# A softmax with relative position bias: one DMA queue and hand-placed pieces, against a queue for loads and a queue for stores

## The chip, the cores and the metric

The kernel runs on one core of a Trainium2 chip. The metric is the device time of one execution in microseconds; the median of several runs counts. The chip's core has a VectorE (DVE), a ScalarE (ACT), a GpSimd (POOL), a TensorE (PE, not used here), a SyncE (SP) that here only issues transfers, and 16 DMA engines, which move data between HBM and the on-chip memory (SBUF) for all of them.

## The reference

```python
B, H, S, max_rel = 2, 8, 2112, 16
logits: [B, H, S, S] f32        rel_bias: [H, 2 * max_rel + 1] f32
rel = clip(pos[:, None] - pos[None, :], -max_rel, max_rel) + max_rel
logits = logits + rel_bias[:, rel][None]
logits = logits - logits.max(axis=-1, keepdims=True)
exp = np.exp(logits)
return exp / exp.sum(axis=-1, keepdims=True)
```

There are 2 x 8 x 2112 = 33,792 rows of 2112 numbers. Each is read once and written once: 285.5 MB each way.

## The kernel before

Partition p of the 128 owns 264 neighbouring rows (`ROWS`), so one head's 2112 rows lie on 8 partitions. The rows are worked through in 44 chunks (`N`) of 6 rows per partition (`R`); a chunk is one load of 128 x 50,688 bytes and one store of the same size. There are four buffers, X0 to X3 (`NBUF`), and chunk n uses buffer n mod 4. Only the rows around the diagonal see a bias that is not constant. A strip of it for four chunks is copied out of PSUM (`M`) into `F`.

For each chunk VectorE adds the bias and takes the negative maximum of each row (`add`), ScalarE takes the exponential with its sum (`exps`), and VectorE, after every three rows (`HALF`), forms the reciprocals and scales (`scale`). VectorE does add and scale of a chunk before it goes on to the next. `take(eng, sem, n)` makes an engine wait for a semaphore and count it down. `ld[b]` says that a load has landed in buffer b, `st[b]` that its store has landed, `scaled` counts scaled rows.

SyncE issues all large transfers, in an order that is written out: the loads of chunks 0 to 3, the store of chunk 0, and then in a loop the store of chunk k+1 (after its scales) and the load of chunk k+4 (after the store of chunk k has landed). The transfers share one queue, in that order.

Two chunks are stored otherwise. Of chunk 0, rows 0 and 1 of each partition are left out of the main store (line 300). Lines 290 to 295 (`parts`) issue eight small transfers for part of them, each with one partition per DMA engine on fewer or more engines (`AHEAD`), and GpSimd stores the rest by five indirect transfers (`pieces`, line 165), whose rows are picked out by index lists that it builds (`choose`). A piece is 2 rows, 16.9 KB. Of chunk 41 the last three rows are treated likewise (`BEHIND` and `LAST`), in pieces of 25.3 KB. So some DMA engines store a few pieces more, others fewer. GpSimd waits for `ready` before each set, and SyncE waits for `soft` at the end. The last chunk is stored in two halves, on `landed`.

Of the kernel before, what the change touches and what calls it, by code (L numbers as in the profile page):

```python
# [8 lines left out]
I32 = mybir.dt.int32  # L9
EXP = mybir.ActivationFunctionType.Exp  # L10
ALU = mybir.AluOpType
ENG = mybir.EngineType
# [3 lines left out]
def kernel(  # L16
# [6 lines left out]
    nc = tc.nc  # L23
    P = 128
    B, H, S, S2 = logits.shape
# [3 lines left out]
    ROWS = B * H * S // P  # L29
    PB = S // ROWS  # L30
    assert ROWS * P == B * H * S and PB * ROWS == S and PB == H == 8
    R = 6
    NBUF = 4
    STEP = R * NBUF
    N = ROWS // R
    HALF = R // 2
# [1 line left out]
    MW = S + ROWS - 1  # L38
    FW = S + STEP - 1
    BIG = 3.0e38  # L40
    LOW, HIGH = 32, 96
    A0, A1 = 0, 2
    AHEAD = [(LOW + i, 16 - 2 * i) for i in range(4)] + [(i, 8) for i in range(4)]
    FIRST = [
# [5 lines left out]
    ]  # L50
    Z0, Z1 = HALF, R
    BEHIND = [(LOW + i, 16) for i in range(4)]
    LAST = [
        (80, 0, 1, []),
        (48, 80, 1, list(range(16, 48))),
# [3 lines left out]
    ]  # L59
    FAR = 1 << 20  # L60
    for own, plan in ((AHEAD, FIRST), (BEHIND, LAST)):
        assert sorted([p + 4 * i for p, k in own for i in range(k)]
                      + [p0 + lap * i for n, p0, lap, keep in plan for i in keep]) == list(range(P))

    io = ctx.enter_context(tc.tile_pool(name="io", bufs=1))
    X = [io.tile([P, R * S], FP32, tag=f"X{b}", name=f"X{b}") for b in range(NBUF)]
# [2 lines left out]
    nmax = io.tile([P, STEP], FP32, tag="nmax", name="nmax")  # L69
    tot = io.tile([P, STEP], FP32, tag="tot", name="tot")  # L70
    rec = io.tile([P, STEP], FP32, tag="rec", name="rec")
    sel = io.tile([P, len(FIRST) + len(LAST)], I32, tag="sel", name="sel")
    ip = io.tile([P, 3, PB], I32, tag="ip", name="ip")
    ps = ctx.enter_context(tc.tile_pool(name="ps", bufs=1, space=bass.MemoryType.PSUM))
    M = ps.tile([P, 4096], FP32, tag="M", name="M")
# [5 lines left out]
    def rows(t, j, n):  # L81

        return bass.AP(tensor=t.tensor, offset=t.offset + j * S, ap=[[ROWS * S, P], [1, n * S]])

    with tc.tile_critical(no_gpsimd_drain=True):  # L85
        ld = [nc.alloc_semaphore(f"ld{b}") for b in range(NBUF)]
        st = [nc.alloc_semaphore(f"st{b}") for b in range(NBUF)]
        added = nc.alloc_semaphore("added")
        expd = nc.alloc_semaphore("expd")
        scaled = nc.alloc_semaphore("scaled")  # L90
# [1 line left out]
        rb = nc.alloc_semaphore("rb")  # L92
        idx = nc.alloc_semaphore("idx")
        dve = nc.alloc_semaphore("dve")
        ready = nc.alloc_semaphore("ready")
        pool = nc.alloc_semaphore("pool")
        soft = tc.alloc_semaphore("soft")
        main = nc.alloc_semaphore("main")
        landed = tc.alloc_semaphore("landed")

        def take(eng, sem, n):
            eng.wait_ge(sem, n).then_inc(sem, -n)  # L102


        def load(j, b):
            nc.sync.dma_start(out=X[b][:, :], in_=rows(logits, j, R)).then_inc(ld[b], 16)

        def store(j, b, s0=0, n=R, sem=None):
            take(nc.sync, scaled, n)
            nc.sync.dma_start(  # L110
                out=rows(out, j + s0, n), in_=X[b][:, s0 * S : (s0 + n) * S]
            ).then_inc(sem or st[b], 16)

# [22 lines left out]

        nc.gpsimd.iota(ip[:, 0], pattern=[[0, PB]], base=0, channel_multiplier=1).then_inc(idx, 1)
        nc.gpsimd.iota(ip[:, 2], pattern=[[1, PB]], base=0, channel_multiplier=0).then_inc(idx, 1)
        g = nc.gpsimd
        made = [0]  # L140

        def step(ins):
            made[0] += 1
            ins.then_inc(pool, 1)

        def choose(plan, w, unit, row):

            for n, p0, lap, keep in plan:
                col = sel[:, w : w + 1]
                step(g.iota(col, pattern=[[0, 1]], base=(p0 * ROWS + row) // unit, channel_multiplier=lap * ROWS // unit))  # L150
                a, b = (min(keep), max(keep)) if keep else (P, P)
                cuts = [(-a, 1, ALU.is_ge), (b, -1, ALU.is_ge)]
                cuts += [(-i, 1, ALU.not_equal) for i in range(a, b) if i not in keep]
                for base, mul, op in cuts:
                    g.wait_ge(pool, made[0])
                    step(g.affine_select(out=col, in_=col, pattern=[[0, 1]], base=base, channel_multiplier=mul,  # L156
                                         compare_op=op, fill=float(FAR)))
                w += 1

        def pieces(plan, w, unit, x, r0):  # L160

            blocks = out.rearrange("b h s t -> (b h s t)").rearrange("(n c) -> n c", c=unit * S)
            step_p = list(x.ap[0])[0]
            for n, p0, lap, keep in plan:
                g.indirect_dma_start(  # L165
                    out=blocks, out_offset=bass.IndirectOffsetOnAxis(ap=sel[0:n, w : w + 1], axis=0),
                    in_=bass.AP(tensor=x.tensor, offset=x.offset + p0 * step_p + r0 * S,
                                ap=[[lap * step_p, n], [1, unit * S]]),
                    in_offset=None, bounds_check=P * ROWS // unit - 1, oob_is_err=False,
                ).then_inc(soft, 16)  # L170
                w += 1

        choose(FIRST, 0, A1 - A0, A0)
        take(g, pool, made[0])
        made[0] = 0
        take(g, ready, 1)
        pieces(FIRST, 0, A1 - A0, X[0], A0)
        choose(LAST, len(FIRST), Z1 - Z0, (N - 3) * R + Z0)
        take(g, pool, made[0])
        take(g, main, 16 * (1 + len(AHEAD)))  # L180
        g.wait_ge(soft, 16 * len(FIRST))
        g.sem_inc(st[0], 16)
        take(g, ready, 1)
        pieces(LAST, len(FIRST), Z1 - Z0, X[(N - 3) % NBUF], Z0)

        SC = H * W
        mask = [F[:, SC + i * PB : SC + (i + 1) * PB] for i in range(9)]
        dp, dh, eq, hm, gt, le, lt, ra, rz = mask
# [66 lines left out]
        def exps(b):  # L255
            for r in range(b * R, (b + 1) * R):
                x = X[b][:, (r - b * R) * S : (r - b * R + 1) * S]
                take(nc.scalar, added, 1)
                nc.scalar.activation(  # L259
                    out=x, in_=x, func=EXP, scale=-1.0, bias=nmax[:, r : r + 1],  # L260
                    accum_out=tot[:, r : r + 1],
                ).then_inc(expd, 1)
# [11 lines left out]
        with nc.Fori(0, ROWS - STEP + 1, STEP, engines=[ENG.DVE]) as j:  # L274
            strip(j)
            take(v, dve, 1)
            for b in range(NBUF):
                add(b)
                scale(b)
        with nc.Fori(0, ROWS // STEP, 1, engines=[ENG.Activation]):  # L280
            for b in range(NBUF):
                exps(b)

        def parts(own, x, r0, r1, j, sem):

            step_p = list(x.ap[0])[0]
            for p, k in own:
                nc.sync.dma_start(  # L290
                    out=bass.AP(tensor=out.tensor, offset=out.offset + (p * ROWS + j + r0) * S,
                                ap=[[4 * ROWS * S, k], [1, (r1 - r0) * S]]),
                    in_=bass.AP(tensor=x.tensor, offset=x.offset + p * step_p + r0 * S,
                                ap=[[4 * step_p, k], [1, (r1 - r0) * S]]),
                ).then_inc(sem, 16)

        nc.sync.wait_ge(scaled, HALF)
        nc.sync.sem_inc(ready, 1)
        take(nc.sync, scaled, R)
        nc.sync.dma_start(out=rows(out, A1, R - A1), in_=X[0][:, A1 * S : R * S]).then_inc(main, 16)  # L300
        parts(AHEAD, X[0], A0, A1, 0, main)
        with nc.Fori(0, ROWS - 2 * STEP + 1, STEP, engines=[ENG.SP]) as j:
            for b in range(NBUF):
                store(j + (b + 1) * R, (b + 1) % NBUF)
                take(nc.sync, st[b], 16)
                load(j + (b + NBUF) * R, b)
        take(nc.sync, scaled, R)
        nc.sync.sem_inc(ready, 1)
        late = X[(N - 3) % NBUF]
        nc.sync.dma_start(out=rows(out, (N - 3) * R, Z0), in_=late[:, 0 : Z0 * S]).then_inc(st[(N - 3) % NBUF], 16)  # L310
        parts(BEHIND, late, Z0, Z1, (N - 3) * R, st[(N - 3) % NBUF])
        store((N - 2) * R, (N - 2) % NBUF)
        store((N - 1) * R, (N - 1) % NBUF, 0, HALF, landed)
        store((N - 1) * R, (N - 1) % NBUF, HALF, R - HALF, landed)
        for b in range(NBUF - 1):
            take(nc.sync, st[(N + b) % NBUF], 16 * (1 + len(BEHIND)) if b == 1 else 16)
    nc.sync.wait_ge(soft, nc.sync.to_reg(16 * (len(FIRST) + len(LAST))), synchronizes=[nc.sync.lower_ap(out)])
    nc.sync.wait_ge(landed, nc.sync.to_reg(32), synchronizes=[nc.sync.lower_ap(out)])


# [28 lines left out]
```

## Time and profile before

| | |
|---|---|
| median of 3 runs | 1328.01 us (1327.66 to 1330.19) |
| span of the profiled execution | 1327.4 us |
| VectorE, ScalarE, GpSimd busy | 977.7, 575.2, 56.6 us |
| loads | 44 of 6336 KB, median 44.6 us from issue to landing |
| stores of whole chunks | 41 of 6336 KB, median 52.6 us |
| indirect stores by GpSimd | 10 |

The profiled execution has no time of its own beside its span; the span runs from the first to the last instruction, and the median of the runs is 0.6 us longer. In the page, a row of the costliest groups has line, engine, operation, output and input, count, then busy time and mean nanoseconds, then the idle time before. A queue row has packets, MB and the share of 16 engines' time. L102 is the line in `take`: a wait put down to it is a wait for a semaphore.

### The profile page before, as it was taken

The page shows a single profiled execution, that of the slowest core. Times are in us where ns is not written, and L with a number is a line of the kernel's source. Part 1 is how long each engine was busy: PE and PEld are TensorE (multiplying, and loading weights), DVE is VectorE, ACT ScalarE, POOL GpSimd, SP SyncE. Part 2 cuts the span into 40 slices and gives each one's busy share as a digit, 9 for nine tenths or more (in the row PEclk, how much of TensorE's full clock was granted, in tenths as well). Part 3 has the DMA queues.
Part 4 walks back from the last instruction along what each step waited for, and adds up shares of the span by engine and source line. Part 5 has one row for each costly group of instructions (what it writes and reads, how often), then busy time and mean ns, then how long its engine had stood idle before and what let it go on. Part 6 is the DMA issues. An engine that isn't in the chain of part 4 may idle for free. (4 is left out here: it accounts for less than half of the span.)

```text
span 1327.4 us, 2638 instructions
## 1 busy us (share of the span) xinstructions
DVE 977.7 (74%) x917; ACT 575.2 (43%) x539; POOL 56.6 (4%) x90
## 2 busy tenths in 40 slices
DVE  7998667777877766787777767677877776687763
ACT  3474333444443343344444333444444343345431
POOL 2750000000000000000000000000000000000100
DMA  9999999999999999999999999999999999999998
GB/s 415 410 438 431 435 431 434 434 435 429 432 437 429 431 438 431 428 438 434 429 432 432 435 435 431 432 435 437 429 435 432 437 425 434 438 437 429 428 427 365
DMA packets 13564, 571.01 MB, mean 430 GB/s; under 512 B 1896, under 2 KB 1912, under 8 KB 1912
## 3 DMA queue, kind: packets, MB, share of 16 engines
q1 hardware_dynamic: 13112, 568.59, 99.3%
q0 software_dynamic: 416, 2.37, 0.4%
q14 instruction: 4, 0.03, 0.0%
q10 hardware_dynamic: 32, 0.02, 0.0%
HBM read 285.49 MB, written 288.92 MB: 433 GB/s over the span
## 5 line engine op out<-in xcount | busy, mean ns | idle before, releaser
L250 DVE CUSTOM_DVE_ANT_0 X<-X,F 128x2112 f32<-128x2112 f32 x264 | 605.2, 2354 | 307.2 <-DVEq L102 307.2
L259 ACT ACTIVATE X<-X,nmax 128x2112 f32<-128x2112 f32 x264 | 541.7, 2052 | 541.8 <-ACTq L102 520.1
L271 DVE TENSOR_SCALAR X<-X,rec 128x2112 f32<-128x2112 f32 x264 | 332.4, 1315 | 13.2 <-DVEq L102 0.2
L259 ACT ACT_TABLE_LOAD x11 | 14.1, 1283 | 184.3 <-ACTq L102 184.3
L165 POOL DMA_INDIRECT out_dram<-X,sel x10 | 13.7, 1366 | 1182.5 <-POOLq L102 1180.0
L259 ACT ACTIVATION_READ_ACCUMULATOR X<-X,nmax 128x1 f32 x264 | 49.2, 186 | 0.0
L156 POOL TENSOR_SCALAR_AFFINE_SELECT sel<-sel 128x1 int32<-128x1 int32 x64 | 40.5, 632 | 9.6 <-POOL sel L156 0.5
L244 DVE COPY F<-M 128x2135 f32 x11 | 26.1, 2374 | 0.5 <-DVEq L273 0.5
L250 DVE DVE_READ_ACCUMULATOR2_ANT nmax<- 128x1 f32 x264 | 21.6, 82 | 0.0
L267 DVE RECIPROCAL rec<-tot 128x3 f32<-128x3 f32 x88 | 14.9, 170 | 0.0
L206 DVE TENSOR_TENSOR F<-F 128x264 f32<-128x264 f32 x1 | 0.4, 433 | 7.0 <-DMA F<-in_rel_bias_dram 7.0
L150 POOL IOTA sel<- 128x1 int32 x10 | 2.4, 244 | 0.0
L236 DVE COPY M<-F 128x1848 f32<-128x1848 f32 x1 | 2.1, 2076 | 0.0
L125 DVE MEMSET F<- 128x264 f32 x1 | 0.3, 278 | 1.1 <-SPq L85 1.1
L210 DVE TENSOR_REDUCE F<-F 128x33 f32<-128x264 f32 x1 | 0.6, 606 | 0.0
L233 DVE TENSOR_TENSOR M<-F 128x264 f32<-128x264 f32 x1 | 0.4, 441 | 0.0
L225 DVE TENSOR_TENSOR F<-F,rbS 128x264 f32<-128x264 f32 x1 | 0.4, 428 | 0.0
L203 DVE TENSOR_SCALAR F<-F 128x8 f32<-128x8 f32 x4 | 0.4, 165 | 0.0
L238 DVE COPY M<-rbS 128x247 f32<-128x247 f32 x1 | 0.4, 405 | 0.0
L213 DVE STREAM_TRANSPOSE F<-F 128x64 f32<-128x64 f32 x1 | 0.2, 246 | 0.0
L218 DVE STREAM_TRANSPOSE F<-F 128x64 f32<-128x64 f32 x1 | 0.2, 245 | 0.0
L223 DVE TENSOR_SCALAR F<-F,rbS 128x8 f32<-128x8 f32 x1 | 0.2, 231 | 0.0
(18 smaller groups left out, 2.8 us busy)
## 6 DMA issues: line engine op xcount, KB each, us to landing
X<-in_logits_dram SPq DMA_DIRECT2D x44, 6336.0 KB, 44.6
out_dram<-X SPq DMA_DIRECT2D x41, 6336.0 KB, 52.6
out_dram<-X SPq DMA_DIRECT2D x3, 3168.0 KB, 19.2
out_dram<-X SPq DMA_DIRECT2D x1, 4224.0 KB
out_dram<-X SPq DMA_DIRECT2D x4, 396.0 KB, 48.5
out_dram<-X SPq DMA_DIRECT2D x4, 132.0 KB
out_dram<-X SPq DMA_DIRECT2D x1, 264.0 KB
out_dram<-X SPq DMA_DIRECT2D x1, 231.0 KB
```

The lines of the kernel that those rows point to most:

```text
L150: step(g.iota(col, pattern=[[0, 1]], base=(p0 * ROWS + row) // unit, channel_multiplier=lap * ROWS // unit))
L156: step(g.affine_select(out=col, in_=col, pattern=[[0, 1]], base=base, channel_multiplier=mul, compare_op=op, fill=float(FAR)))
L165: g.indirect_dma_start(out=blocks, out_offset=bass.IndirectOffsetOnAxis(ap=sel[0:n, w : w + 1], axis=0), in_=bass.AP(tensor=x.tensor, offs ...
L203: then(v.tensor_scalar(out=m, in0=dp, scalar1=0.0, scalar2=None, op0=op))
L206: then(v.tensor_tensor(out=view(F, 0, [[W, H], [1, W]]), in0=view(F, 0, [[W, H], [1, W]]), in1=view(F, SC + 3 * PB, [[1, H], [0, W]]), op= ...
L210: then(v.tensor_reduce(out=F[:, RB : RB + W], in_=view(F, 0, [[1, W], [W, H]]), axis=mybir.AxisListType.X, op=ALU.add))
L236: then(v.tensor_copy(out=view(M, U + W, [[ROWS, PB], [1, ROWS - W]]), in_=view(F, SC + 7 * PB, [[1, PB], [0, ROWS - W]])))
L244: v.tensor_copy(out=F[:, :], in_=M[:, bass.ds(ROWS - STEP - j, FW)]).then_inc(dve, 1)
L250: v.tensor_tensor_reduce(out=x, in0=x, in1=F[:, STEP - 1 - r : STEP - 1 - r + S], scale=-1.0, scalar=BIG, op0=ALU.add, op1=ALU.min, accum_ ...
L259: nc.scalar.activation(out=x, in_=x, func=EXP, scale=-1.0, bias=nmax[:, r : r + 1], accum_out=tot[:, r : r + 1],).then_inc(expd, 1)
L267: v.reciprocal(out=rec[:, r0 : r0 + HALF], in_=tot[:, r0 : r0 + HALF]).then_inc(inv, 1)
L271: v.tensor_scalar_mul(out=x, in0=x, scalar1=rec[:, r : r + 1]).then_inc(scaled, 1)
```

## The change

Stores are issued by ScalarE, on its own queue, each after the exponentials of its chunk and after a wait for its scales. SyncE issues loads alone, each after the store of its buffer has landed. The tables, the index lists, the indirect stores and the small transfers are gone; all chunks but the last are stored by one transfer. In the diff the tables are cut to a line each.

```diff
-    AHEAD = [(LOW + i, 16 - 2 * i) for i in range(4)] + [(i, 8) for i in range(4)]
-    FIRST = [
-        (16, 75, 2, [0, 2, 4, 8, 9, 10]),
...
-    BEHIND = [(LOW + i, 16) for i in range(4)]
-    LAST = [
-        (80, 0, 1, []),
...
-    sel = io.tile([P, len(FIRST) + len(LAST)], I32, tag="sel", name="sel")
...
         def store(j, b, s0=0, n=R, sem=None):
-            take(nc.sync, scaled, n)
-            nc.sync.dma_start(
+            take(nc.scalar, scaled, n)
+            nc.scalar.dma_start(
                 out=rows(out, j + s0, n), in_=X[b][:, s0 * S : (s0 + n) * S]
             ).then_inc(sem or st[b], 16)
...
-        choose(FIRST, 0, A1 - A0, A0)
-        take(g, pool, made[0])
-        made[0] = 0
-        take(g, ready, 1)
-        pieces(FIRST, 0, A1 - A0, X[0], A0)
-        choose(LAST, len(FIRST), Z1 - Z0, (N - 3) * R + Z0)
...
-        pieces(LAST, len(FIRST), Z1 - Z0, X[(N - 3) % NBUF], Z0)
...
-        with nc.Fori(0, ROWS // STEP, 1, engines=[ENG.Activation]):
+        with nc.Fori(0, ROWS - 2 * STEP + 1, STEP, engines=[ENG.Activation]) as j:
             for b in range(NBUF):
                 exps(b)
...
-        nc.sync.dma_start(out=rows(out, A1, R - A1), in_=X[0][:, A1 * S : R * S]).then_inc(main, 16)
-        parts(AHEAD, X[0], A0, A1, 0, main)
-        with nc.Fori(0, ROWS - 2 * STEP + 1, STEP, engines=[ENG.SP]) as j:
+                store(j + b * R, b)
+        for n in range(N - NBUF, N):
+            exps(n % NBUF)
+            if n < N - 1:
+                store(n * R, n % NBUF)
+            else:
+                store(n * R, n % NBUF, 0, HALF, landed)
+                store(n * R, n % NBUF, HALF, R - HALF, landed)
+
+        with nc.Fori(STEP, ROWS - STEP + 1, STEP, engines=[ENG.SP]) as j:
             for b in range(NBUF):
-                store(j + (b + 1) * R, (b + 1) % NBUF)
                 take(nc.sync, st[b], 16)
-                load(j + (b + NBUF) * R, b)
-        take(nc.sync, scaled, R)
-        nc.sync.sem_inc(ready, 1)
...
-        parts(BEHIND, late, Z0, Z1, (N - 3) * R, st[(N - 3) % NBUF])
-        store((N - 2) * R, (N - 2) % NBUF)
-        store((N - 1) * R, (N - 1) % NBUF, 0, HALF, landed)
-        store((N - 1) * R, (N - 1) % NBUF, HALF, R - HALF, landed)
+                load(j + b * R, b)
```

SyncE before, from its first stores into its loop (X_58 to X_61 are the buffers X0 to X3; a row's line number is that of its kernel):

```order
L300 DMA out_dram<-X_58 128x8448
L290 DMA out_dram<-X_58 16x4224
L290 DMA out_dram<-X_58 14x4224
L290 DMA out_dram<-X_58 12x4224
L290 DMA out_dram<-X_58 10x4224
L290 DMA out_dram<-X_58 8x4224 x4
L302 UNCONDITIONAL_BRANCH
L110 ISA
L110 DMA out_dram<-X_59 128x12672
L106 ISA
L106 DMA X_58<-in_logits_dram 128x12672
```

The same place on SyncE now:

```order
L217 UNCONDITIONAL_BRANCH
L78 ISA
L78 DMA X_58<-in_logits_dram 128x12672
L78 ISA
L78 DMA X_59<-in_logits_dram 128x12672
L78 ISA
L78 DMA X_60<-in_logits_dram 128x12672
```

Stores no longer stand between the loads, and the small transfers ahead of the loop are gone.

ScalarE's loop before:

```order
L259 ACT_TABLE_LOAD
L259 ACTIVATE X_58,tot<-X_58,nmax 128x2112 x6
L259 ACTIVATE X_59,tot<-X_59,nmax 128x2112 x6
L259 ACTIVATE X_60,tot<-X_60,nmax 128x2112 x6
L259 ACTIVATE X_61,tot<-X_61,nmax 128x2112 x6
```

And ScalarE's loop now:

```order
L184 ACT_TABLE_LOAD
L184 ACTIVATE X_58,tot<-X_58,nmax 128x2112 x6
L82 ISA
L82 DMA out_dram<-X_58 128x12672
L184 ACTIVATE X_59,tot<-X_59,nmax 128x2112 x6
L82 ISA
L82 DMA out_dram<-X_59 128x12672
L184 ACTIVATE X_60,tot<-X_60,nmax 128x2112 x6
```

Each chunk's store stands behind its six exps, with its wait for the scales (the L82 ISA row) ahead of it and the next chunk's exps behind.

More of the change, by code (lines that the diff above doesn't have):

```diff
@@ L40 @@
     BIG = 3.0e38
-    LOW, HIGH = 32, 96
-    A0, A1 = 0, 2
-    AHEAD = [(LOW + i, 16 - 2 * i) for i in range(4)] + [(i, 8) for i in range(4)]
-    FIRST = [
[5 rows of a table removed]
-    ]
-    Z0, Z1 = HALF, R
-    BEHIND = [(LOW + i, 16) for i in range(4)]
-    LAST = [
-        (80, 0, 1, []),
-        (48, 80, 1, list(range(16, 48))),
[3 rows of a table removed]
[L59 to L63, printed above, removed]
     io = ctx.enter_context(tc.tile_pool(name="io", bufs=1))
@@ L94 @@
         dve = nc.alloc_semaphore("dve")
[L95 to L98, printed above, removed]
         landed = tc.alloc_semaphore("landed")
@@ L138 @@
         nc.gpsimd.iota(ip[:, 2], pattern=[[1, PB]], base=0, channel_multiplier=0).then_inc(idx, 1)
[L139 to L171, printed above, removed]
-        choose(FIRST, 0, A1 - A0, A0)
-        take(g, pool, made[0])
-        made[0] = 0
-        take(g, ready, 1)
-        pieces(FIRST, 0, A1 - A0, X[0], A0)
-        choose(LAST, len(FIRST), Z1 - Z0, (N - 3) * R + Z0)
[L179 to L183, printed above, removed]
-        pieces(LAST, len(FIRST), Z1 - Z0, X[(N - 3) % NBUF], Z0)
         SC = H * W
@@ L279 @@
                 scale(b)
-        with nc.Fori(0, ROWS // STEP, 1, engines=[ENG.Activation]):
+        with nc.Fori(0, ROWS - 2 * STEP + 1, STEP, engines=[ENG.Activation]) as j:
             for b in range(NBUF):
                 exps(b)
[L286 to L295, printed above, removed]
@@ L297 @@
-        nc.sync.wait_ge(scaled, HALF)
-        nc.sync.sem_inc(ready, 1)
-        take(nc.sync, scaled, R)
-        nc.sync.dma_start(out=rows(out, A1, R - A1), in_=X[0][:, A1 * S : R * S]).then_inc(main, 16)
-        parts(AHEAD, X[0], A0, A1, 0, main)
-        with nc.Fori(0, ROWS - 2 * STEP + 1, STEP, engines=[ENG.SP]) as j:
+                store(j + b * R, b)
[6 more added lines that the diff above has]
+                store(n * R, n % NBUF, HALF, R - HALF, landed)
@@ L303 @@
+        with nc.Fori(STEP, ROWS - STEP + 1, STEP, engines=[ENG.SP]) as j:
             for b in range(NBUF):
-                store(j + (b + 1) * R, (b + 1) % NBUF)
                 take(nc.sync, st[b], 16)
-                load(j + (b + NBUF) * R, b)
[L307 to L310, printed above, removed]
-        parts(BEHIND, late, Z0, Z1, (N - 3) * R, st[(N - 3) % NBUF])
@@ L312 @@
-        store((N - 2) * R, (N - 2) % NBUF)
-        store((N - 1) * R, (N - 1) % NBUF, 0, HALF, landed)
-        store((N - 1) * R, (N - 1) % NBUF, HALF, R - HALF, landed)
+                load(j + b * R, b)
         for b in range(NBUF - 1):
-            take(nc.sync, st[(N + b) % NBUF], 16 * (1 + len(BEHIND)) if b == 1 else 16)
-    nc.sync.wait_ge(soft, nc.sync.to_reg(16 * (len(FIRST) + len(LAST))), synchronizes=[nc.sync.lower_ap(out)])
+            take(nc.sync, st[b], 16)
     nc.sync.wait_ge(landed, nc.sync.to_reg(32), synchronizes=[nc.sync.lower_ap(out)])
```

7 rows, old and new, of tables (FIRST, LAST) are left out of this document.

## Prediction

> **What bounds the kernel now.** I began with the page: the span, the engines' busy time, the DMA row and the queues.
>
> ```profile
> span 1327.4 us, 2638 instructions
> DVE 977.7 (74%) x917; ACT 575.2 (43%) x539; POOL 56.6 (4%) x90
> DMA  9999999999999999999999999999999999999998
> q1 hardware_dynamic: 13112, 568.59, 99.3%
> q0 software_dynamic: 416, 2.37, 0.4%
> HBM read 285.49 MB, written 288.92 MB: 433 GB/s over the span
> ```
>
> No compute engine is above 74%, while the 16 DMA engines are full in every slice. SyncE's queue (q1) carries 568.59 MB and GpSimd's (q0) 2.37 MB. Next, the busy time by windows; the last two columns are the DMA share and GB/s.
>
> ```profile
> 0.00:2.00 2.00, 0.84 (x7) 0.00 (x0) 0.85 (x9) 1.00 0.09 25
> 80.00:1240.00 1160.00, 862.14 (x793) 510.01 (x478) 5.78 (x6) 1.00 1.00 433
> 1318.00:1320.00 2.00, 0.00 (x0) 0.00 (x0) 0.00 (x0) 1.00 1.03 444
> 1320.00:1325.00 5.00, 0.00 (x0) 0.00 (x0) 0.00 (x0) 1.00 0.60 259
> 1325.00:1327.40 2.40, 0.00 (x0) 0.00 (x0) 0.00 (x0) 1.00 0.00 0
> ```
>
> Nearly nothing moves before 2 us. From 80 to 1240 us the engines never rest, and move 433 GB/s. At the end they don't stop together: after 1320 they have 0.60 x 5 = 3.0 us of packets left on average, but not evenly. SyncE's waits, and the row of its last wait by line (start from and to), show when the last one lands.
>
> ```profile
> SPq L102 <- SPq L102: 1217.5, 85, 29.9
> SPq L318 <- DMA out_dram<-X: 13.9, 1, 13.9
> ```
> ```profile
> L318 SPq EVENT_SEMAPHORE  x1: 17/17/17, 1326.3 to 1326.3; - x1
> ```
>
> The last store has landed at 1326.3. The 1217.5 us are SyncE waiting for scales and for stores to land before it may go on, while the engines stay full: the queue is fed ahead of need. So the time is the bytes, over the rate of 16 engines, plus whatever makes one engine finish after the others. VectorE has slack everywhere (307.2 us of idle time before its adds):
>
> ```profile
> L250 DVE CUSTOM_DVE_ANT_0 X<-X,F 128x2112 f32<-128x2112 f32 x264 | 605.2, 2354 | 307.2 <-DVEq L102 307.2
> ```
>
> Three things can then change the time: the rate at which an engine works through its packets, the evenness at the end, and an engine running dry.
>
> **The change, part by part.** *The compute chain and the issue of stores.* These are the rows of the first chunk, from the timeline.
>
> ```profile
> 0.96 1.99 SPq L106 DMA_DIRECT2D X<-in_logits_dram  x4
> 18.99 2.36 DVE L250 CUSTOM_DVE_ANT_0 X<-X,F 128x2112 f32<-128x2112 f32 x1 [0.59 <-DVEq L102]
> 32.99 3.78 DVE L271 TENSOR_SCALAR X<-X,rec 128x2112 f32<-128x2112 f32 x3
> 37.01 3.78 DVE L271 TENSOR_SCALAR X<-X,rec 128x2112 f32<-128x2112 f32 x3 [0.15 <-DVEq L102]
> 40.70 2.35 DVE L250 CUSTOM_DVE_ANT_0 X<-X,F 128x2112 f32<-128x2112 f32 x1
> 40.88 0.34 SPq L300 DMA_DIRECT2D out_dram<-X  x1
> 43.19 2.06 ACT L259 ACTIVATE X<-X,nmax 128x2112 f32<-128x2112 f32 x1 [8.08 <-ACTq L102]
> ```
>
> A chunk takes VectorE 40.79 - 18.99 = 21.8 us (17.8 to the end of its first half). The added wait makes ScalarE stand still until the chunk is scaled; queued behind it are the exps of the next chunk. The first of these needs the next chunk's first add, which starts at 40.70 and ends at 43.05. ScalarE has sat idle for 8.08 us before that exp, and one store issue costs 0.34 us (SyncE's row), so it is over by about 41.3. Cost nothing; without the add in between it would be 0.34 us per chunk, hidden by VectorE's slack.
>
> *The loads.* Before, a load stood behind a store's issue on SyncE. The timeline in mid-run shows that it was not held up by that:
>
> ```profile
> 583.62 0.34 SPq L110 DMA_DIRECT2D out_dram<-X  x1
> 606.55 0.34 SPq L106 DMA_DIRECT2D X<-in_logits_dram  x1
> ```
>
> The store is issued at 583.62; the load behind it goes 23 us later, when the buffer's own store has landed. That wait stays. Gain nothing.
>
> *Two queues instead of one.* Before, an engine does its eight packets of a load, then its eight of a store. After, it holds both and must choose at each packet. What that costs, the trace shows only where GpSimd's stores ran beside SyncE's loads. The DMA view gives packets, MB and the engines' share; MB divided by share x 16 x window is the rate of a busy engine. Here are 100 to 460 us (q1 alone), 1080 to 1240 (q1 alone), 50 to 62 and 1260 to 1283 (both queues), and 40 to 50 (both, while the first pieces are issued).
>
> ```profile
> q1 hardware_dynamic: 3456, 155.72, 100.2%
> ```
> ```profile
> q1 hardware_dynamic: 1550, 69.65, 100.6%
> ```
> ```profile
> q1 hardware_dynamic: 90, 4.56, 88.0%
> q0 software_dynamic: 90, 0.51, 10.1%
> ```
> ```profile
> q1 hardware_dynamic: 199, 8.03, 83.3%
> q0 software_dynamic: 141, 1.42, 15.5%
> ```
> ```profile
> q1 hardware_dynamic: 96, 4.06, 101.3%
> q0 software_dynamic: 64, 0.24, 5.8%
> ```
>
> The rates are 26.98, 27.05, 26.91, 25.99 and 25.09 GB/s. Against the best, 27.05, the two-queue windows lose 0.5% of 188 engine-us (0.95 us), 3.9% of 364 (14.3 us) and 7.2% of 171 (12.4 us). In 50 to 62 us q0 moved 0.51 MB in pieces of 16.9 KB, thirty of them: 32 ns for each store put between loads. In 1260 to 1283 it moved 1.42 MB in pieces of 25.3 KB, fifty-six: 255 ns each. The early one-queue window loses 0.25% of 5772 engine-us, 14.6 us, over 12 turns from load to store on 16 engines: 76 ns a turn. I read these as one price, paid where an engine turns from one direction to the other. Its ends are 0 (1080 to 1240, with five turns an engine and no loss) and 255 ns. I take 50 ns, between 32 (nearest: two queues, whole packets, nothing being issued) and 76.
>
> How many turns? Loads are issued at 0.96 and start at 2 us, and an engine does a packet of 50.7 KB at 27.05 GB/s in 1.875 us, the eight of a load in 15.0. The first store, issued after 40.8, begins at about 42 us, so 21 of its 352 load packets are through; the other 331 run beside stores. 331 x 50 ns = 16.5 us. Before had 44 turns: 2.2 us. Net +14.3 us, with ends -2.2 and +82.
>
> [...]
>
> [...]
>
> *The balancing pieces.* Their disturbance goes: 12.4 and 14.3 engine-us, over 16 engines 0.8 + 0.9 = 1.7 us. What they level goes too. Before, engines that all stopped together would stop at 1320 + 3.0 + 0.47 (half of a 0.94-us packet in flight) = 1323.5; the last landed at 1326.3. So 2.8 us of unevenness are left with the pieces. Without them it lies between 0 (all engines have equal bytes) and 2.8 + 2.5: the first plan gives an engine up to four pieces of 0.63 us more or less. I take 1.8, a gain of 1.0.
>
> *The end.* The last chunk's load must land early enough that stores cover its compute. In turns, each queue has half an engine. At 42 us loads have 20.5 us of work left in the queue, store 0 has 15: it ends at 72, load 3 at about 84, and so on every 30 us, loads 12 us behind stores. The last load ends with 15 - 12/2 = 9 us of one store left and 15 of the next, 24 us. The first half-store needs 0.6 + 17.8 + 1.1 = 19.5. Covered by 4.5 us: cost nothing.
>
> *Sum.* 1327.4 - 1.7 - 1.0 + 14.3 = 1339.0. The median of the runs stands 0.6 us above this span: **1339.6 us**.
>
> **The rivals.** *Turns are free.* [...] For it: 1080 to 1240 us lose nothing, and an engine that alternates may settle into a rhythm. Against: all windows with two queues are slower. 1327.4 - 1.7 - 1.0 + 0.6 = 1325.3, down to 1323.1 if the old turns vanish too, and up to 1329 with the worst evenness.
>
> *The store queue runs ahead.* If engines favoured stores, stores would be flushed as computed, and the last chunk's compute would lie bare: store 42 is ready 8 us before the last load lands and is done 7 us after it, the first half-store comes at 19.5. Price 12.5 us, deciding once loads lag more than 21 us: 1325.3 + 12.5 = 1338 with free turns, 1352 otherwise. Against it: equal packets and 12 us of lag.
>
> *Every turn costs what the late window cost.* 331 x 255 ns = 84 us: 1408. Against it: the window from 50 to 62 us has the same mixture at an eighth of the price.
>
> **How the numbers follow.** Paid turns (32 to 120 ns, 1333 to 1362) 0.50; free 0.36; stores ahead 0.08; the dear turn 0.06. The prediction is the likeliest, 1339.6. The range runs from 1324 to 1360: it leaves out the dear turn, the tip of the first case and the lower end of the second; the likeliest case alone has 1333 to 1362. A measurement here can tell about 0.2%, 2.7 us. Free turns split into faster 0.20 and same 0.16; the others are slower, 0.64.
>
> **What would show it.** Right: a DMA share of 1.00 in mid-run with 427 to 430 GB/s instead of 433, and an end as even as before. Wrong: 433 GB/s in mid-run (free turns); a gap in the DMA row near 1300 us while VectorE works on the last chunk (stores ahead); exps that start later after the add than now (ScalarE's wait).

## The result and the profile after

The changed kernel takes 1334.12 us (median of 6, 1330.35 to 1337.95), the kernel before beside it 1328.0. The ratio is 1.0041, with an interval of 1.0027 to 1.0056: slower by 5 to 6 us, where 11.6 us were forecast. The runs fall into two groups, 1330 to 1332 and 1336 to 1338, and this belongs to the result: it comes back below in profiles of one and the same program. The profiled execution took 1331.85 us, its span is 1330.0. The page, in the order in which it was shown of before:

```profile
span 1330.0 us, 2473 instructions
DVE 977.7 (74%) x917; ACT 574.3 (43%) x538; POOL 0.4 (0%) x6
q1 hardware_dynamic: 6336, 285.48, 49.8%
q10 hardware_dynamic: 6512, 285.49, 49.6%
HBM read 285.49 MB, written 285.47 MB: 429 GB/s over the span
```

The change does what it says: q1 has the loads, q10 (ScalarE's) the stores, in equal shares, and GpSimd is idle. Next the windows (engines' busy time, DMA share, GB/s):

```profile
80.00:1240.00 1160.00, 855.10 (x786) 504.95 (x473) 0.00 (x0) 1.00 1.00 434
1300.00:1318.00 18.00, 9.59 (x10) 4.00 (x4) 0.00 (x0) 1.00 0.88 376
1318.00:1320.00 2.00, 0.00 (x0) 0.00 (x0) 0.00 (x0) 1.00 0.94 406
1320.00:1325.00 5.00, 0.00 (x0) 0.00 (x0) 0.00 (x0) 1.00 0.45 193
1325.00:1327.00 2.00, 0.00 (x0) 0.00 (x0) 0.00 (x0) 1.00 0.06 25
1327.00:1330.00 3.00, 0.00 (x0) 0.00 (x0) 0.00 (x0) 1.00 0.02 8
```

In mid-run 434 GB/s instead of 433: the alternation of loads and stores costs nothing that shows in the rate. The loss shows at the end. From 1300 to 1318 us the share falls to 0.88 while VectorE still works on the last chunk (9.59 us of the window), where before had 0.96 and 6.87 us; and from 1325 on about one engine of 16 (0.06) works alone for 3 us. The timeline of VectorE shows when the last chunk could begin, after a wait of 8.13 us for its load, and when its first half was scaled:

```profile
1288.10 2.36 DVE L175 CUSTOM_DVE_ANT_0 X<-X,F 128x2112 f32<-128x2112 f32 x1 [8.13 <-DVEq L74]
1302.10 3.78 DVE L196 TENSOR_SCALAR X<-X,rec 128x2112 f32<-128x2112 f32 x3
```

The same window and the same first add in the kernel before, where the last chunk began 2.9 us earlier:

```profile
1300.00:1318.00 18.00, 6.87 (x7) 1.27 (x2) 0.00 (x0) 1.00 0.96 414
1285.23 2.36 DVE L250 CUSTOM_DVE_ANT_0 X<-X,F 128x2112 f32<-128x2112 f32 x1 [12.53 <-DVEq L102]
```

The packet records of the trace (start and duration of each packet; the chains of the 16 engines are put together from packets that follow one another) say who waited. Most engines have stored chunk 42 by 1305.0 to 1305.5 and stand idle until 1306.8, when the scales of the last chunk's first half let its store start. They all stop at 1322.0. One engine stops 2.3 us after them and one 6.7 us after them:

```
           mean end of 16   last engine's end   span
before        1323.4            1325.9         1327.4
after         1322.6            1328.7         1330.0
```

The mean end is 0.8 us earlier than before, although most engines now idle for about 1.5 us. The last engine ends 6.1 us after the mean instead of 2.5.

SyncE's waits and ScalarE's timeline at the first store bear on two more points of the prediction, the loads and ScalarE's wait:

```profile
SPq L74 <- SPq L74: 1286.8, 43, 72.8
SPq L223 <- DMA out_dram<-X: 14.5, 1, 14.5
```
```profile
40.99 0.38 ACTq L82 DMA_DIRECT2D out_dram<-X  x1
43.14 2.06 ACT L184 ACTIVATE X<-X,nmax 128x2112 f32<-128x2112 f32 x1 [8.07 <-ACTq L74]
```

The first exp of the second chunk starts at 43.14 (43.19 before), after 8.07 us of idle time (8.08): ScalarE's wait for the scales costs nothing. SyncE still spends nearly the whole run waiting for stores to land before it may load (1286.8 us; 1217.5 before), so taking the stores off its queue gains nothing.

### The profile page after: what moved, and what is told of

It reads as the page before. It is cut to its first block, busy times and chain, and to the rows that moved or that the text cites. A ratio compares the mean times of both kernels' runs of the same rounds, so it can differ in the third digit from the quotient of the medians.

```text
span 1330.0 us, 2473 instructions
## 1 busy us (share of the span) xinstructions
DVE 977.7 (74%) x917; ACT 574.3 (43%) x538; POOL 0.4 (0%) x6
## 3 DMA queue, kind: packets, MB, share of 16 engines
q1 hardware_dynamic: 6336, 285.48, 49.8%
q10 hardware_dynamic: 6512, 285.49, 49.6%
## 5 line engine op out<-in xcount | busy, mean ns | idle before, releaser
L184 ACT ACT_TABLE_LOAD x10 | 12.8, 1283 | 170.8 <-ACTq L74 170.8
## 6 DMA issues: line engine op xcount, KB each, us to landing
F<-in_rel_bias_dram ACTq DMA_DIRECT2D x1, 16.5 KB, 8.0
```

The source lines that it names most:

```text
L184: nc.scalar.activation(out=x, in_=x, func=EXP, scale=-1.0, bias=nmax[:, r : r + 1], accum_out=tot[:, r : r + 1],).then_inc(expd, 1)
```

## The experiments

Four theories were put to the test. **Evenness** (called U): the pieces level engines that were disturbed, so their loss is what costs. **Queues** (Q): two queues make one engine fall behind, whatever the pieces do. **Out of step** (R): any engine can fall ever further behind once it is out of step with a group of engines in step, and engines that start scattered are safe from it. **Own disturbance** (P): a certain engine is slower by itself.

### The two parts of the change apart

e1 keeps the one queue of before and drops the pieces; e2 takes the two queues and keeps the pieces.

```diff
 e1, against after
-            take(nc.scalar, scaled, n)
-            nc.scalar.dma_start(
+            take(nc.sync, scaled, n)
+            nc.sync.dma_start(
...
+        store(0, 0)
+        with nc.Fori(0, ROWS - 2 * STEP + 1, STEP, engines=[ENG.SP]) as j:
+            for b in range(NBUF):
+                store(j + (b + 1) * R, (b + 1) % NBUF)
                 take(nc.sync, st[b], 16)
+                load(j + (b + NBUF) * R, b)
 e2, against before
-            take(nc.sync, scaled, n)
-            nc.sync.dma_start(
+            take(nc.scalar, scaled, n)
+            nc.scalar.dma_start(
...
             for b in range(NBUF):
-                store(j + (b + 1) * R, (b + 1) % NBUF)
+                exps(b)
+                store(j + b * R, b)
...
```

> The kernel before on its one queue and in its order, but without the pieces: chunks 0 and 41 are stored by one transfer like the others. Theory U (what is lost is evenness: every DMA engine has the same bytes, one or two are disturbed more than the others, and only the pieces took work off them): as slow as the changed kernel or nearly, 1330 to 1336 us, with a DMA share after 1320 us that trails off on one or two engines. Rival Q (two queues on an engine let one engine fall behind; with one queue all keep step): within 1 us of before, 1327 to 1329.

> The changed kernel's two queues, with the pieces of before put back: the small transfers on ScalarE's queue, the indirect ones on GpSimd's. Theory U: the pieces make up for the disturbed engine, so 1326 to 1329 us, like before or 1 to 2 us under it, since mid-run is as fast as before. Rival Q: the lag of one engine is made by two queues and grows to 6 us whatever the start, so 1329 to 1336 us.

Measured: e1 1331.23 us (9 runs, 1329.44 to 1333.73), ratio 1.0027 (1.0017 to 1.0037). e2 1334.22 us (8 runs, 1329.39 to 1339.06), ratio 1.0044 (1.0022 to 1.0067). Their windows, e1 first:

```profile
80.00:1240.00 1160.00, 857.31 (x788) 507.86 (x476) 0.00 (x0) 1.00 1.00 433
1320.00:1325.00 5.00, 0.00 (x0) 0.00 (x0) 0.00 (x0) 1.00 0.32 137
1325.00:1330.00 5.00, 0.00 (x0) 0.00 (x0) 0.00 (x0) 1.00 0.15 66
```
```profile
80.00:1240.00 1160.00, 848.14 (x779) 490.27 (x459) 0.83 (x1) 1.00 1.00 433
1310.00:1320.00 10.00, 6.25 (x6) 0.65 (x2) 0.00 (x0) 1.00 0.76 327
1330.00:1335.00 5.00, 0.00 (x0) 0.00 (x0) 0.00 (x0) 1.00 0.06 25
```

Both move 433 GB/s in mid-run, so neither part touches the rate. With one queue and no pieces, eleven engines stop by 1320.6 and five trail behind them, to 1330.4. With two queues one engine trails, pieces or not, and the other 15 also idle before the last chunk (share 0.76 from 1310 to 1320). The pieces are worth 3.6 us with one queue (1331.23 against 1327.62). With two, the kernel with pieces has 1334.22 and the kernel after, run beside it (e0, below), 1336.32: 2.1 us, not clear of the noise, for e2's own runs lie between 1329 and 1339. Either part alone costs time, and both end in stragglers. U expected e1 as it came out, Q expected e2 so; neither expected both.

### What the pieces do for one queue

x1 is the kernel before with the pieces of chunk 0 alone, x2 with those of chunk 41 alone.

```diff
 x1
-        take(nc.sync, scaled, R)
-        nc.sync.sem_inc(ready, 1)
-        late = X[(N - 3) % NBUF]
-        nc.sync.dma_start(out=rows(out, (N - 3) * R, Z0), in_=late[:, 0 : Z0 * S]).then_inc(st[(N - 3) % NBUF], 16)
-        parts(BEHIND, late, Z0, Z1, (N - 3) * R, st[(N - 3) % NBUF])
+        store((N - 3) * R, (N - 3) % NBUF)
...
 x2
-        nc.sync.dma_start(out=rows(out, A1, R - A1), in_=X[0][:, A1 * S : R * S]).then_inc(main, 16)
-        parts(AHEAD, X[0], A0, A1, 0, main)
+        store(0, 0)
...
```

> The kernel before with the pieces of chunk 0 alone; chunk 41 is stored by one transfer. Chunk 0's pieces put the engines 4.4 us apart at the start and leave them with unequal bytes. Theory R (what the pieces buy is that no group of engines runs in step): about before, 1327 to 1330 us, since nothing grows afterwards. Rival U (the pieces level the end): no better than the one-queue kernel without pieces, 1330 to 1333 us.

> The kernel before with the pieces of chunk 41 alone; chunk 0 is stored by one transfer, so the engines start in step. Theory R: like the one-queue kernel without pieces, 1330 to 1333 us. Rival U: about before, 1327 to 1329 us.

x1: 1329.8 us (10 runs), ratio 1.0007 (0.9998 to 1.0017), no different from before. x2: 1333.66 us (5 runs), ratio 1.0039 (1.0024 to 1.0053), no better than with no pieces. Their last windows, x1 first:

```profile
1320.00:1325.00 5.00, 0.00 (x0) 0.00 (x0) 0.00 (x0) 1.00 0.37 157
1325.00:1330.00 5.00, 0.00 (x0) 0.00 (x0) 0.00 (x0) 1.00 0.02 7
```
```profile
1320.00:1325.00 5.00, 0.00 (x0) 0.00 (x0) 0.00 (x0) 1.00 0.74 319
1325.00:1330.00 5.00, 0.00 (x0) 0.00 (x0) 0.00 (x0) 1.00 0.13 56
```

So the pieces at the start do all of it that can be told from noise. They don't level the end; they set the engines off some 4.5 us apart (4.7 in x1 at 150 us, 6.5 at 1230, by the landings), where without pieces the gap from first to last grows from 3.2 to 10.1 us (e1). The next table shows it: the time that the slowest engine has lost against the median engine (the ninth of 16), in us, worked out from the moments at which each engine's share of each transfer landed. With two queues an engine serves two transfers at a time, and the number is the mean of its lag in the load and in the store.

```
                                 150     510     870    1230 us
before (one queue, pieces)       1.5     2.3     2.7     2.0
x1 (one queue, first pieces)     1.4     2.0     2.3     3.6
e1 (one queue, no pieces)        2.8     6.6     9.3     9.8
x9 (one queue, engine 0 pushed)  2.3     5.7     7.5     7.7
after (two queues)               0.8     2.0     3.6     8.5
e0 (the same kernel)             1.8     6.8    11.5    11.5
m1 (the same, with marks)        1.2     5.6    11.8    12.9
m1b (the same as m1)             1.5     3.8     4.0     5.2
e2 (two queues, pieces)          2.8     6.2    10.2    13.1
```

Without scatter a straggler loses by this table 0.1 to 0.5 us in every 30 us (a load and a store), until it is 8 to 13 us behind; then e0, e1, m1 and x9 lose little or nothing more. That is theory R for one queue. For two queues R's last part falls: e2 starts scattered (5.6 us at 150 us) and its slowest engine runs away all the same, as Q says.

### The same program, two outcomes

e0 is the kernel after once more. m1 and m1b are one program: after, with 15 tiny loads of 15 to 1 partitions behind the last load, so that the engines can be numbered by how many each has: the one with all 15 is called engine 0, the one with none engine 15 (m2 and m3: the same with e1 and with before). The small transfers of the kernel before fall that way: of the 84 packets of its transfers of 16, 14, 12, 10 and four times 8 partitions, eight engines have 8 each and two engines each 4, 3, 2 and 1, by the chains.

```diff
+        for k in range(15, 0, -1):
+            nc.sync.dma_start(
+                out=mk[0:k, 4 * (k - 1) : 4 * k],
+                in_=bass.AP(tensor=logits.tensor, offset=logits.offset, ap=[[ROWS * S, k], [1, 4]]),
+            ).then_inc(mark, 16)
```

> The changed kernel itself on this chip, as the mark for the other three: 1330 to 1338 us by its six runs so far. Theory U and rival Q both expect a DMA share of 1.00 and 433 to 434 GB/s in mid-run, and one or two engines that end 2 to 10 us after the rest.

> The changed kernel with fifteen tiny loads of 15, 14, ... 1 partitions behind its last load, on SyncE's queue: a load of k partitions runs on DMA engines 0 to k-1, so engine e lands 15 - e of them, and the engine that is behind can be told by its count. Time within 1 us of the changed kernel, 1331 to 1338 us. Theory U, one engine that is disturbed by its place: the engine behind is one that the plans of before ease (12 to 15). Rival R, any engine can fall behind once it is out of step with the others: another number.

> The same kernel a second time. Theory U: the same engine is behind. Rival R: a different engine is behind, or the amount differs by more than 5 us.

e0: 1336.32 us (4 runs), ratio 1.0065 (1.0048 to 1.0082). m1: 1337.63. m1b: 1328.85, and so 8.8 us less for the same program. The start of the last chunk's first add, in the timelines of e0, m1 and m1b:

```profile
1293.98 2.36 DVE L175 CUSTOM_DVE_ANT_0 X<-X,F 128x2112 f32<-128x2112 f32 x1 [8.14 <-DVEq L74]
```
```profile
1293.88 2.36 DVE L177 CUSTOM_DVE_ANT_0 X<-X,F 128x2112 f32<-128x2112 f32 x1 [8.14 <-DVEq L76]
```
```profile
1285.18 2.36 DVE L177 CUSTOM_DVE_ANT_0 X<-X,F 128x2112 f32<-128x2112 f32 x1 [8.12 <-DVEq L76]
```

The last windows of e0, m1 and m1b:

```profile
1310.00:1320.00 10.00, 5.63 (x6) 0.02 (x1) 0.00 (x0) 1.00 0.78 332
1325.00:1330.00 5.00, 0.00 (x0) 0.00 (x0) 0.00 (x0) 1.00 0.59 253
1330.00:1335.00 5.00, 0.00 (x0) 0.00 (x0) 0.00 (x0) 1.00 0.05 20
```
```profile
1310.00:1320.00 10.00, 5.53 (x6) 0.00 (x0) 0.00 (x0) 1.00 0.78 332
1330.00:1335.00 5.00, 0.00 (x0) 0.00 (x0) 0.00 (x0) 1.00 0.05 20
```
```profile
1310.00:1320.00 10.00, 0.00 (x0) 0.00 (x0) 0.00 (x0) 1.00 0.97 418
1320.00:1325.00 5.00, 0.00 (x0) 0.00 (x0) 0.00 (x0) 1.00 0.18 76
```

The straggler sets this time: the last load has landed when its share has. In e0 that is at 1293.9; 18.7 us later (compute of half a chunk, and its store's issue) the other 15 engines, idle for about 5 us, start on the last store at 1312.7 and end at 1327.9 (their packets), and the straggler ends at 1334.6. In m1b no engine ran away, the add starts 8.7 us earlier, the stores of chunk 42 cover the compute, and the last engines end at 1323.9, 1324.0 and 1325.6.

The packet records also show where the straggler loses its time. A packet of a whole transfer takes 1.87 us (median). Some load packets take longer, mostly 2.0 to 2.5 us (in the profiled execution of after, from 100 to 1200 us, 73 of 4684 take over 1.9 us, 45 of them 2.0 to 2.5 us); stores hardly ever do (7 of 4715). The table has, for each engine, the load packets of over 1.9 us and what its load packets took above 1.872 us in all:

```
                        the straggler      each other engine
e0, 350 to 720 us       25, 6.7 us         1 to 7, 0.1 to 1.3 us
m1, 450 to 1000 us      38, 8.4 us         2 to 9, 0.2 to 2.5 us
before, 100 to 1200 us  (none)             4 to 14, 1.3 to 3.3 us
```

In m1 from 1000 to 1240 us, when the straggler falls no further behind, no engine has more than two of them. So one engine takes most of the long packets while it runs away, and in the kernel before all engines take their part. From 100 to 1200 us all packets of whole transfers together lose 36.9 engine-us in before and 20.1 in the profiled execution of after: the sum is no larger, it falls on one engine.

In m1 the straggler has no tiny load, which makes it engine 15, the last in the order. x8 pushes engine 0 out of step by one extra packet of 50.7 KB at the start; x9 does so with one queue.

```diff
+        nc.sync.dma_start(
+            out=X[NBUF - 1][0:1, :],
+            in_=bass.AP(tensor=logits.tensor, offset=logits.offset, ap=[[ROWS * S, 1], [1, R * S]]),
+        ).then_inc(pushed, 16)
-        for n in range(NBUF):
+        for n in range(NBUF - 1):
             load(n * R, n)
+        take(nc.sync, pushed, 16)
+        load((NBUF - 1) * R, NBUF - 1)
```

> The one-queue kernel without the pieces, with the same tiny loads behind its last store. 1330 to 1334 us. Theory U: the engines that are behind are 12 to 15, by 4 to 10 us. Rival R: engines of other numbers are among them.

> The kernel before with the same tiny loads behind its last store. 1327 to 1331 us. The plans give engine 0 four pieces more in chunk 0 and engine 15 four fewer, 2.5 us each way, and by the second plan up to two pieces of 0.94 us less. Theory U: engines 12 to 15 end with the others, within 2 us, although they have 0.9 to 1.6 us less to do. Rival R: the engines end in the order of what the plans give them, engine 0 last.

> The changed kernel with the tiny loads of before, and one more load ahead of all others: one partition of 50.7 KB, which runs on DMA engine 0 alone and puts it 1.9 us behind the other fifteen from the start. Theory R (engines in step hardly lose time; one that is out of step loses more and more): engine 0, the one with fifteen tiny loads, is the last at the end, by 5 us or more, 1333 to 1338 us. Rival P (an engine falls behind by its own disturbances, whatever its start): engine 0 stays 1.9 us behind, and another engine is the last or none.

> The one-queue kernel without pieces, with the tiny loads and with the same extra load on engine 0. Theory R: engine 0 is among the last, 5 to 10 us behind the group, 1331 to 1336 us. Rival P: engine 0 keeps its 1.9 us and the others spread as without the push.

m2 took 1334.64 us, m3 1331.04, x8 1336.66, x9 1334.26 (one run each). Engines behind the group, by number, with their ends, by the packet records:

```
m2 (one queue)          14: 1324.4   4: 1324.7   9: 1326.6   15: 1327.0   1: 1328.2   3: 1329.2
x9 (one queue, push)     1: 1325.1   4: 1325.8  15: 1327.1    3: 1327.8   0: 1328.2
m3 (before)              all between 1321.1 (11) and 1326.0 (8); 3: 1321.2, among the first
m1, x8 (two queues)     15: 1334.5 and 1333.4; the other fifteen by 1327.9 and 1326.7
```

With one queue the push makes engine 0, which is not among the stragglers of m2, the very last: being out of step is enough (R). Engines 1, 3, 4 and 15 straggle in both, so the choice is not pure chance either, and engine 3 is among the first in the kernel before, whose first pieces set it elsewhere. R's own forecast for m3 failed: engine 0, which the plans give the most pieces, ends at 1323.1 in the middle, and 8 is last. With two queues the pushed engine 0 doesn't run away, and 15 does again, which does not fit R and would be a chance of one in sixteen. P, for engine 15, would fit m1 and x8, but not m1b, where no engine ran away in the same program.

### A miss: easing the late engine in the first store

e3 stores two rows of chunk 0 by one transfer of 120 and one of 8 partitions, meant to take bytes off engine 15 at the start; that they do was the author's estimate.

```diff
+        EASE, FEW = 2, 15
+        exps(0)
+        take(nc.scalar, scaled, R)
+        some(0, P, EASE, R)
+        some(0, 8 * FEW, 0, EASE)
+        some(8 * FEW, P - 8 * FEW, 0, EASE)
...
```

> [...] Theory U with the last-numbered engine as the disturbed one: 3 to 5 us under the changed kernel beside it, 1326 to 1331 us. Theory U with another engine as the disturbed one, or rival Q with whichever engine: no gain, 0 to 1 us over the changed kernel.

1332.65 us (7 runs, 1331.89 to 1340.83), ratio 1.0048 (1.0029 to 1.0067). In the profile the transfer of 120 partitions itself put the engines up to 6 us apart, so more than one thing was changed. The scatter stayed, nothing ran away in that execution (4.9 us at 1230 us), and the last engine still landed 5.1 us behind the median: not a clean test.

### Two more misses: splitting a load

To see whether engine 15's lag is the whole price, y1 loads the last chunk so that engine 15 gets one packet instead of eight, an estimate by the way the small transfers of before fall; y2 splits the load as often, with equal bytes; y3 is y1 at chunk 3. y4 to y6 are the same with partitions eight apart.

```diff
+            else:
+                load_in(n * R, n % NBUF, CUTS)
 CUTS: transfers of so many neighbouring partitions, or (first, distance, number)
 y1  [16] + [15] * 7 + [7]            y2  [16] * 8       y3  as y1, for chunk 3
 y4  [(0, 8, 16)] + [(i, 8, 15) for i in range(1, 8)] + [(121, 1, 7)]
 y5  [(i, 8, 16) for i in range(8)]                      y6  as y4, for chunk 3
```

> The kernel after, but the last chunk is loaded by nine transfers of 16, seven times 15 and 7 partitions: engine 15 gets one packet of it instead of eight (13.1 us less), engines 0 to 6 one more (1.9 us). If it is engine 15 that falls behind with two queues: the last chunk's scales no longer come late, the 13 to 14 engines of the group no longer stand idle before it, and all end within 6 us of each other: span 1326 to 1328, time 1328 to 1330 in every execution. If it is another engine each time: as the kernel after, up to 1.9 us slower, 1331 to 1339, with one engine 6 to 7 us behind the group.

> The kernel after, but the last chunk is loaded by eight transfers of 16 partitions, one packet of each for every engine: equal bytes, only the split of y1. Both theories: as the kernel after, 1331 to 1338; any gain of y1 over this one is engine 15's seven packets. If the split itself levels the engines: near y1.

> As y1, but in the load of chunk 3, at the start; with the tiny transfers behind the last load that tell an engine's number by their count. Engine 15 starts 13.1 us ahead. If it is slower by itself with two queues (13 to 15 us lost by 1230 us), it is back with the group at the end: 1328 to 1330. If an engine loses because it is behind a group, engine 15 stays ahead and ends 10 us or more before the others, and another one may fall behind: 1328 to 1338. If it loses because it is out of step, ahead or behind, it drifts towards the group.

> The kernel after, but the last chunk is loaded by nine transfers: one of 16 and seven of 15 partitions, eight apart, and one of the 7 left, 121 to 127. Engine 15 gets one packet of it instead of eight (13.1 us less), engines 0 to 6 one more (1.9 us). If engine 15's lag is what two queues cost: the others no longer stand idle before the last chunk's scales and all end within 6 us of each other, span 1326 to 1328, time 1328 to 1330 in every execution. If another engine lags, or several: as y5, 1331 to 1339.

> [...] All theories: as the kernel after, 1331 to 1338, load packets of 1.87 us. If the number of transfers, and not neighbouring partitions, made the first split slow: 1354 to 1366.

> As y4, but in the load of chunk 3, with the tiny transfers behind the last load that tell an engine's number by their count. Engine 15 starts 13.1 us ahead. If it loses 13 us by itself over the run with two queues: back with the group, 1328 to 1330. If it loses because it is behind: it stays ahead, another engine may lag, 1328 to 1338. If engines out of step disturb one another in every packet, as in the split of neighbouring partitions (2.03 us a packet at 600 to 700 us): over 1400.

Medians: y1 1368.73, y2 1364.36, y3 1532.32, y4 1350.63, y5 1350.14, y6 1502.91 us (four executions each; y6 from 1349.35 to 1519.5). The splits cost more than what they were to test. Windows of y2 and of y5, 1255 to 1275 us, when the split load runs:

```profile
1255.00:1275.00 20.00, 11.18 (x9) 8.29 (x7) 0.00 (x0) 1.00 1.00 274
```
```profile
1255.00:1275.00 20.00, 12.45 (x11) 9.44 (x9) 0.00 (x0) 1.00 0.99 340
```

The engines are full and yet move 274 and 340 GB/s. By the packet records a load packet there takes 5.0 us (median, neighbouring partitions) and 3.3 us (eight apart) instead of 1.87; the stores beside them stay near 1.9 us. That y4 isn't faster than y5 says nothing of engine 15: the last load landed so late that VectorE waited 28.12 us for it in y5, as its timeline shows, and a lag of 8 us disappears under that.

```profile
1312.46 2.36 DVE L190 CUSTOM_DVE_ANT_0 X<-X,F 128x2112 f32<-128x2112 f32 x1 [28.12 <-DVEq L75]
```

y5 itself was expected at 1331 to 1338 with load packets of 1.87 us, so spreading the partitions did not make a split harmless.

What y3 and y6 show is that a disturbance early on can stay to the end: y6, in three of its four executions, runs like the one profiled, at 388 GB/s and a share of 0.93 over the whole middle (its windows, below). One engine's share of the stores lands 28.7 us and its share of the loads 47.5 us after the median around 500 us, and 28.6 and 47.2 us around 1230. Both kernels carry the tiny loads, which tell the numbers: in y6 ten of them come after all others, so it is engine 5; in y3 twelve and eleven, engines 3 and 4. Engine 15, which by the same estimate had seven packets of 1.87 us, 13.1 us, less to load at the start, is not the one in either.

```profile
80.00:1240.00 1160.00, 741.14 (x681) 435.87 (x408) 0.00 (x0) 1.00 0.93 388
```

Easing engine 15 by a split over partitions four apart, as before's own small transfers have them (16.9 KB in 0.63 us, median, stores), was not tried.

## Why the prediction was wrong

**The step that failed** is the price of the turns, "331 x 50 ns = 16.5 us", net +14.3 us. It measured nothing: 434 GB/s against 433 from 80 to 1240 us, and 433 in e2 and e0; e2 has the turns and the pieces and still has 433. The loss of the window from 100 to 460 us, read as 76 ns a turn, did sit at the turns, but in a few long packets and not in all: 58 of its 3072 packets take over 5% more than 1.872 us and hold 14.2 of 16.4 engine-us, and of the 55 whose place in their transfer could be told each is the last of a load's eight, just ahead of a turn. What the prediction had no reason for was to multiply this by the number of turns. After, with a turn at about 87% of the packets from 100 to 1200 us (by the chains), 73 of 4684 load packets take over 1.9 us. The other windows on which the price rested (50 to 62, 40 to 50 and 1260 to 1283 us) did run slower, at 26.91, 25.09 and 25.99 GB/s a busy engine against 27.05, but the alternation of directions, which the changed kernel has all the way, is not what made them so. Each had small pieces in flight or being issued; which of the two it was, no run took apart. The prediction itself had a window that said 0, and gave it the other end of a range instead of the rival.

**The balancing pieces.** "I take 1.8, a gain of 1.0" had the wrong sign. That part took unevenness for something fixed by bytes and early disturbances, from 0 to 5.3 us. It grows during the run. In the profiled execution the last engine ends 6.1 us after the mean of all, where 1.8 were set and before has 2.5; the other part of it, 1.7 us of disturbance saved, fits a mean end that is 0.8 us earlier in spite of some 1.5 us of idling.

**The end**, "Covered by 4.5 us: cost nothing", fails by the same cause. The cover was worked out for engines in step, and for the median engine it nearly held: its share of the last load landed at 1283.1 us and of chunk 42's store at 1305.6, 22.5 us where 24 were worked out. Half an engine for each queue, from which these were worked out, is what the profile of after shows (49.8% and 49.6%). But the last load has landed only with the slowest. A straggler 8.5 us late in the profiled execution uncovers about 1.5 us, one of 11.5 us in e0 about 5 us. The rival with the bare compute named this symptom, a share that falls near 1300 us while VectorE works on the last chunk, but not the cause: the store queue doesn't run ahead of the loads, one engine runs behind the others in both.

**What was right**: ScalarE's wait costs nothing, the loads gain nothing, and the sign. But the sign was luck: it was right for a wrong reason. The rival with free turns had the rate, and its 1325.3, "up to 1329 with the worst evenness", had the same hole as the forecast. Closed by the records: the span grows from 1327.4 to 1330.0 as the mean end falls by 0.8 us, the last engine's distance to it grows by 3.6 us, and what follows the last packet is 0.2 us shorter. In e0 the mean end is 1328.3 (5 us of idling) and the straggler 6.3 us after it: 1335.9.

**What stays open.** The runs show that one engine falls behind, when, in which packets, by how much and what that costs at the end. Why those load packets take longer, why mostly on an engine that is out of step, why this stops at 8 to 13 us in most runs, and why with two queues and whole loads it was engine 15 in both executions whose straggler carries a number (m1 and x8), they don't show. With two queues neither a scattered start nor one in step tells the outcome: e2 is scattered and ran away, e3 is scattered and did not, and m1 and m1b are one program. With one queue engine 15 fell behind in m2 and x9 too, there as one of six and of five stragglers.

## What to carry to other kernels

When a profile shows 16 full DMA engines, look at what each of them has done, not at the mean: the rate may be perfect and the time still be set by one engine that has fallen behind by half a transfer, at the last load and again at the last store. Small odd transfers at the start of a tuned kernel may be there to set engines apart, so take them out alone and measure before you take them out with something else. A loss that you find at some event need not be a price of every such event: look at the single packets before you multiply it by a count. Where one program's runs fall in two groups, profile it until you have one of each; the difference of the two is the cheapest experiment there is.

## What was not expected of the hardware

Loads and stores that alternate on two queues, at about 87% of the packets, run at 434 GB/s, no slower than eight and eight on one queue at 433. One program took 1337.63 and 1328.85 us, by whether one engine of 16 ran away from a group in step. And a transfer over 16 partitions, one packet for each engine, was far slower than the same packets in a transfer over 128: 274 GB/s (neighbouring partitions) and 340 (eight apart) against 418 in the same window of after, with load packets of 5.0, 3.3 and 1.87 us. Why, no run here isolates.
